# Skewness of 1024 rows: one reduce for two sums, two small ScalarE steps moved, and new transfer sizes

## Chip, cores, metric

One core of a Trainium2 chip. The metric is the device time of one execution in microseconds (us). All runs quoted here were fast (one core, granted TensorE clock 0.94 to 0.99).

Engines: PE is TensorE, PEld its weight loads, DVE is VectorE, ACT is ScalarE, POOL is GpSimd, SP is the queue that issues the transfers. In the profile lines, a bracket at the end names the idle time of the engine before the instruction and what ended it; `prof` prints it only where that idle time is above 0.15 us.

## The reference

```python
# x: 1024 x 8192 float32
mean = np.mean(x, axis=-1, keepdims=True)
std = np.std(x, axis=-1, keepdims=True)
z = (x - mean) / (std + 1e-8)
return np.mean(z ** 3, axis=-1)
```

The kernel gets it from three raw sums a row: of x, of x squared and of x cubed. 1024 rows are 8 blocks of 128 rows, numbered 0 to 7. A block is loaded in several transfers, called units here and counted from 0, as in the code (the prediction counts them from one: its "unit six" is unit 5).

## The kernel before

```python
UNITS = [                                    # columns of each transfer, by block
    [4096, 4096], [4096, 4096], [4096, 4096], [4096, 4096],
    [3072, 2944, 2176],
    [2944, 2688, 2560],
    [1664, 1536, 1664, 1792, 1536],
    [1024, 1152, 768, 1024, 1024, 1280, 1024, 896],
]
X_BUFS = 8                                   # so many transfers may be in flight or in use
...
s2u = small("s2u", NB * K); s3u = small("s3u", NB * K)     # partial sums, a column a slice
...
    def first_sums():                        # blocks 0 to 5, run in block 6
        for dst, src in ((m2a, s2u), (m3a, s3u)):
            v.tensor_reduce(out=dst, in_=src[:, 0 : F * K].rearrange("p (b c) -> p b c", c=K),
                            axis=X_AXIS, op=ALU.add)
        ...                                  # small ScalarE and GpSimd steps
    at(F - 2, 0, lambda: v.tensor_tensor(    # first means, in block 4
        out=m1a[:, 0:nw], in0=s1ps[:, 0:nw], in1=s1a, op=ALU.add))
    ...
    def mid_sums():                          # block 6, run in block 7: two reduces again
        ...
    def third_1(o):                          # "v"
        act(out=o["v3"], in_=o["m1sq"], func=AF.Identity, scale=-2.0 / 3.0, bias=o["m2"])
    def third_2(o):                          # "t"
        act(out=o["t"], in_=o["v3"], func=AF.Identity, scale=o["nm1"], bias=o["m3"])
    at(L, 4, lambda: third_1(mid))           # after unit 4 of the last block
    at(L, 5, lambda: third_2(mid))           # after unit 5
    at(L, 5, lambda: g.tensor_tensor(out=skew[:, F : F + 1], ...))

    for b, widths in enumerate(UNITS):
        for k, w in enumerate(widths):
            ...
            loads.append(nc.sync.dma_start(out=xt, in_=xv[b, :, c0 : c0 + w]))
            for s, e in _slices(b, w):
                ...
                act(out=sq, in_=xt[:, s:e], func=AF.Square, scale=s_scale,
                    accum_out=s2u[:, j : j + 1])                       # squares: ScalarE
                v.scalar_tensor_tensor(out=cube, in0=sq, scalar=1.0, in1=xt[:, s:e],
                    op0=ALU.mult, op1=ALU.mult, accum_out=s3u[:, j : j + 1])   # cubes: VectorE
            ...
            for c in range(n):                                         # sum of x: TensorE
                nc.tensor.matmul(out=tp, lhsT=xt[:, c * P : (c + 1) * P], rhs=ident,
                                 ..., is_transpose=True)
            for fn in todo.pop((b, k), ()):
                fn()                                                   # the small steps above
    copy_sums(L)                             # last block: ScalarE copy, then closing formulas
    ...
    third_2(o)
    v.tensor_scalar(out=skew[:, L:NB], in0=s3u[:, j - 1 : j], scalar1=o["t"], scalar2=o["rr"],
                    op0=ALU.add, op1=ALU.mult)                         # the last instruction
```

Of the kernel before, what the change touches and what calls it, by code (L numbers as in the profile page):

```python
# [10 lines left out]
ALU = mybir.AluOpType  # L11
# [3 lines left out]
X_AXIS = mybir.AxisListType.X  # L15
# [2 lines left out]
UNITS = [  # L18
    [4096, 4096],
    [4096, 4096],  # L20
    [4096, 4096],
    [4096, 4096],
    [3072, 2944, 2176],
    [2944, 2688, 2560],
    [1664, 1536, 1664, 1792, 1536],
    [1024, 1152, 768, 1024, 1024, 1280, 1024, 896],
]
S1_ACT = {(0, 0): 1024, (1, 0): 1024, (2, 0): 1024}
SUB_MAX = 2304
# [7 lines left out]
def _slices(b, w):  # L37
    n = -(-w // (SUB_WIDE if b >= 2 and w >= WIDE else SUB_MAX))
    step = -(-w // n // 128) * 128
    return [(s, min(s + step, w)) for s in range(0, w, step)]  # L40
# [3 lines left out]
def kernel(  # L44
# [5 lines left out]
    nc = tc.nc  # L50
# [5 lines left out]
    NB = R // P  # L56
    L = NB - 1
    F = EARLY
# [4 lines left out]
    nw = len(S1_ACT)  # L63
# [7 lines left out]
    n_sl = [sum(len(_slices(b, w)) for w in u) for b, u in enumerate(UNITS)]  # L71
    K = max(n_sl)
# [7 lines left out]
    def small(name, n):  # L80
        return onep.tile([P, n], FP, tag=name, name=name)
# [4 lines left out]
    nc.scalar.activation(out=tiny, in_=onesn, func=AF.Square)  # L86
    ident = small("ident", P)
    make_identity(nc, ident)
    s2u = small("s2u", NB * K)
    s3u = small("s3u", NB * K)  # L90
    nc.vector.memset(s2u, 0.0)
    nc.vector.memset(s3u, 0.0)
    s1a = small("s1a", nw)
    same = small("same", max(S1_ACT.values()))
    junk = small("junk", K)
# [7 lines left out]
    act, g, v = nc.scalar.activation, nc.gpsimd, nc.vector  # L103
# [4 lines left out]
    def at(b, k, fn):  # L108
        todo.setdefault((b, k), []).append(fn)
# [9 lines left out]
    for b in range(L):  # L119
# [1 line left out]
        at(b + 1, 0, lambda b=b: mean(b))  # L121


    m2a, m3a, m1sqa, m1sq3a, nm1a, vara, rra = (
        small(f"{t}a", F) for t in ("m2", "m3", "m1sq", "m1sq3", "nm1", "var", "rr")
    )

    def first_sums():
        for dst, src in ((m2a, s2u), (m3a, s3u)):
            v.tensor_reduce(  # L130
                out=dst, in_=src[:, 0 : F * K].rearrange("p (b c) -> p b c", c=K),
                axis=X_AXIS, op=ALU.add,
            )
        nc.scalar.copy(out=m1a[:, nw:F], in_=s1ps[:, nw:F])
        act(out=m1sqa, in_=m1a, func=AF.Square)
        g.tensor_tensor(out=vara, in0=m2a, in1=m1sqa, op=ALU.subtract)  # L136
        g.tensor_tensor(out=rra, in0=vara, in1=expo, op=ALU.pow)  # L137

    def first_rest():
# [4 lines left out]
        g.tensor_tensor(out=m3a, in0=m3a, in1=m1sq3a, op=ALU.add)  # L144
        g.tensor_tensor(out=skew[:, 0:F], in0=m3a, in1=rra, op=ALU.mult)  # L145

    at(F - 2, 0, lambda: v.tensor_tensor(
        out=m1a[:, 0:nw], in0=s1ps[:, 0:nw], in1=s1a, op=ALU.add))
    at(F, 1, first_sums)
    at(F, 2, first_rest)  # L150


    names = ("m2", "m3", "m1sq", "nm1", "var", "v3", "rr", "t")
    mid, end = ({t: small(f"{t}_{b}", 1) for t in names} for b in (F, L))

    def mid_sums():
        for t, src in (("m2", s2u), ("m3", s3u)):
            v.tensor_reduce(
                out=mid[t], in_=src[:, F * K : F * K + n_sl[F]], axis=X_AXIS, op=ALU.add
            )  # L160

    def mid_power():
        act(out=mid["m1sq"], in_=s1ps[:, F : F + 1], func=AF.Square)
# [4 lines left out]
    def third_1(o):  # L168
        act(out=o["v3"], in_=o["m1sq"], func=AF.Identity, scale=-2.0 / 3.0, bias=o["m2"])  # L169

    def third_2(o):
        act(out=o["t"], in_=o["v3"], func=AF.Identity, scale=o["nm1"], bias=o["m3"])  # L172

    at(L, 0, mid_sums)
    at(L, 1, mid_power)
    at(L, 4, lambda: third_1(mid))
    at(L, 5, lambda: third_2(mid))
    at(L, 5, lambda: g.tensor_tensor(  # L178
        out=skew[:, F : F + 1], in0=mid["t"], in1=mid["rr"], op=ALU.mult))

    for b, widths in enumerate(UNITS):
# [3 lines left out]
        for k, w in enumerate(widths):  # L185
# [4 lines left out]
            for s, e in _slices(b, w):  # L190
                if last_unit:
                    sq = psum1.tile([P, e - s], FP, tag="sqps", name="sqps")
                else:
                    sq = sqpool.tile([P, e - s], FP, tag="sq", name=f"sq_{b}_{k}_{s}")
                act(  # L195
                    out=sq, in_=xt[:, s:e], func=AF.Square, scale=s_scale,
# [4 lines left out]
                    out=cube, in0=sq, scalar=1.0, in1=xt[:, s:e],  # L201
# [4 lines left out]
            if w_act:  # L206
                act(  # L207
                    out=same[:, 0:w_act], in_=xt[:, w - w_act : w], func=AF.Copy,
# [3 lines left out]
            for c in range(n):  # L212
                nc.tensor.matmul(  # L213
                    out=tp, lhsT=xt[:, c * P : (c + 1) * P], rhs=ident,
# [10 lines left out]
    def row_sum(out, src, n):  # L225
# [13 lines left out]
        out=skew[:, L:NB], in0=s3u[:, j - 1 : j], scalar1=o["t"], scalar2=o["rr"],  # L239
# [37 lines left out]
```

## Time and profile before

| | before |
|---|---|
| median of the runs | 91.14 us (91.05 to 91.33, 6 runs) |
| span of the profiled run | 89.4 us |
| DVE, ACT busy | 73.5, 72.6 us |
| last transfer's landing | 83.66 us |
| ScalarE copy of the last block starts | 84.93 us |
| last cube ends | 86.53 us |
| last instruction starts | 86.85 us |

The landings in this document are read from the semaphore records of the trace; no view prints them, but a ScalarE start that waited for a transfer follows its landing by 0.08 us (unit 5: landing 81.33, start 81.41). Since the end hangs on the last landing and that moves by some tenths between executions, most comparisons below count from it: copy at +1.27, end of the last cube at +2.87, last instruction at +3.19 us. Times are taken to 0.01 us, so a difference of two can be off by 0.01.

The two pairs of reduces, which the change touches, in the VectorE timeline of before (start, length, instruction):

```profile
71.37 0.20 DVE L130 TENSOR_REDUCE m2a<-s2u 128x6 f32<-128x48 f32 x1
71.48 0.19 DVE L130 TENSOR_REDUCE m3a<-s3u 128x6 f32<-128x48 f32 x1
71.59 1.88 DVE L200 SCALAR_TENSOR_TENSOR sq<-sq,x 128x1664 f32<-128x1664 f32 x1
73.40 0.08 DVE L200 DVE_READ_ACCUMULATOR sq<-sq,x 128x1 f32 x1
73.53 2.03 DVE L200 SCALAR_TENSOR_TENSOR sq<-sq,x 128x1792 f32<-128x1792 f32 x1
...
78.31 0.15 DVE L158 TENSOR_REDUCE m<-s2u 128x1 f32<-128x5 f32 x1
78.38 0.15 DVE L158 TENSOR_REDUCE m<-s3u 128x1 f32<-128x5 f32 x1
78.44 1.35 DVE L200 SCALAR_TENSOR_TENSOR sq<-sq,x 128x1152 f32<-128x1152 f32 x1
```

A pair costs from its first start to the start of what follows: 0.22 and 0.13 us. A cube that waits for nothing starts together with the accumulator read of the cube ahead (as at 77.16, 79.71 and 80.59 in this trace). So the cube at 73.53 could have started at 73.40; it waited for its square.

### The profile page before, as it was taken

To read this page: it belongs to the slowest core of one execution; us is meant where nothing else is said; L and a number is where in the kernel's file an instruction comes from. 1 tells how busy PE (TensorE), PEld (TensorE's weight loads), DVE (VectorE), ACT (ScalarE), POOL (GpSimd) and SP (SyncE) were. 2 spreads that over 40 slices of the span, in tenths; PEclk is the share of its full clock that TensorE was granted. 3 is DMA by queue.
4 is the path that set the end of the run, shared out by engine and by line. 5 is a ranking of instruction groups with operands and counts; after the bars stand their busy time and mean duration, and the time that the engine had idled before them with its cause. 6 is when DMAs were issued, how large, how long until landed. Compare 5 with 4: busy or idle time off the path is not lost.

```text
span 89.4 us, 1405 instructions
## 1 busy us (share of the span) xinstructions
PE 62.8 (70%) x504; PEld 58.0 (65%) x504; DVE 73.5 (82%) x97; ACT 72.6 (81%) x120; POOL 13.7 (15%) x18
## 2 busy tenths in 40 slices
PE   0003989492790925999999699489897889897810
PEld 0003969391790915999999598479796778865710
DVE  1000498989989497999989999999999999999980
ACT  6003999599990999989799899499899989998960
POOL 3000000000000000000000000000000089999730
PEclk9999999999999998589999999999999999999999
DMA  4899999999999999999999999999999999996000
GB/s 117 330 403 462 425 425 440 425 425 440 425 433 418 425 433 432 425 433 411 425 424 410 428 435 412 408 429 411 417 416 417 413 406 411 413 403 236 8 0 2
DMA packets 4038, 33.64 MB, mean 376 GB/s; under 512 B 576, under 2 KB 576, under 8 KB 2240
## 3 DMA queue, kind: packets, MB, share of 16 engines
q1 hardware_dynamic: 4032, 33.56, 90.2%
q8 instruction: 4, 0.07, 0.3%
q14 instruction: 2, 0.02, 0.0%
HBM read 33.55 MB, written 0.00 MB: 375 GB/s over the span
## 4 chain that ended last, share of the span: by engine, by line
DMA 58%; DVE 19%; ACT 14%; issue 5%; SPq 1%; PE 0%; ACTq 0%; DVEq 0%
DMA x<-in_x_dram 58%; DVE sq L200 18%; ACT sq L195 9%; ACT same L207 1%; ACT sqps L195 1%; SPq L188 1%; ACT t L172 1%; ACT tsb L112 0%; PE s1ps L115 0%; DVE skew L238 0%; ACT v L169 0%; ACT junk L226 0%; ACT m1sq L231 0%; DVE m2a L130 0%; DVE m3a L130 0%
## 5 line engine op out<-in xcount | busy, mean ns | idle before, releaser
L200 DVE SCALAR_TENSOR_TENSOR sq<-sq,x 128x1408 f32<-128x1408 f32 (+9 forms) x43 | 71.7, 1721 | 12.6 <-ACT sq L195 12.4
L195 ACT ACTIVATE sq<-x 128x1408 f32<-128x1408 f32 (+9 forms) x43 | 62.3, 1451 | 13.1 <-DMA x<-in_x_dram 12.4
L213 PE MATMUL tp<-ident,x 128*128 128x128 f32 x488 | 60.9, 284 | 15.2 <-DMA x<-in_x_dram 15.0
L213 PEld LDWEIGHTS tp<-ident,x 128*128 128x128 f32 x488 | 56.6, 148 | 18.2 <-DMA x<-in_x_dram 10.0
L136 POOL TENSOR_TENSOR vara<-m2a,m1sqa 128x6 f32<-128x6 f32 x1 | 1.8, 1812 | 70.4 <-DVE m3a L130 70.4
L115 PEld LDWEIGHTS s1ps<-onesn,tsb 128*128 128x128 f32 x16 | 2.4, 188 | 9.3 <-ACT tsb L112 9.3
L115 PE MATMUL s1ps<-onesn,tsb 128*128 128x1 f32 x16 | 3.0, 255 | 7.6 <-ACT tsb L112 7.6
L195 ACT ACTIVATION_READ_ACCUMULATOR sq<-x 128x1 f32 x43 | 8.0, 187 | 0.0
L200 DVE DVE_READ_ACCUMULATOR sq<-sq,x 128x1 f32 x43 | 3.6, 83 | 0.0
L137 POOL TENSOR_TENSOR rra<-vara,expo 128x6 f32<-128x6 f32 x1 | 3.1, 3145 | 0.1
L207 ACT ACTIVATE same<-x 128x1024 f32<-128x1024 f32 x3 | 3.1, 1041 | 0.0
L112 ACT COPY tsb<-tp 128x128 f32<-128x128 f32 x8 | 1.9, 242 | 0.0
L86 ACT ACT_TABLE_LOAD x1 | 1.3, 1283 | 0.7 <-PEq L261 0.7
L166 POOL TENSOR_TENSOR rr<-var,expo 128x1 f32<-128x1 f32 x1 | 1.4, 1426 | 0.1
L144 POOL TENSOR_TENSOR m3a<-m3a,m1sq3a 128x6 f32<-128x6 f32 x1 | 1.3, 1330 | 0.1
L165 POOL TENSOR_TENSOR var<-m,m1sq 128x1 f32<-128x1 f32 x1 | 1.2, 1174 | 0.0
L200 DVE SCALAR_TENSOR_TENSOR cube<-sqps,x 128x896 f32<-128x896 f32 x1 | 1.1, 1089 | 0.0
L143 POOL TENSOR_TENSOR m1sq3a<-m1sq3a,nm1a 128x6 f32<-128x6 f32 x1 | 1.1, 1067 | 0.1
L178 POOL TENSOR_TENSOR skew<-t,rr 128x1 f32<-128x1 f32 x1 | 1.0, 976 | 0.1
L195 ACT ACTIVATE sqps<-x 128x896 f32<-128x896 f32 x1 | 0.9, 897 | 0.0
L145 POOL TENSOR_TENSOR skew<-m3a,rra 128x6 f32<-128x6 f32 x1 | 0.8, 799 | 0.1
L172 ACT ACTIVATE t<-v,m,nm 128x1 f32<-128x1 f32 x2 | 0.8, 379 | 0.0
(36 smaller groups left out, 7.5 us busy)
## 6 DMA issues: line engine op xcount, KB each, us to landing
x<-in_x_dram SPq DMA_DIRECT2D x8, 2048.0 KB, 23.4
x<-in_x_dram SPq DMA_DIRECT2D x2, 1472.0 KB, 29.6
x<-in_x_dram SPq DMA_DIRECT2D x4, 512.0 KB, 8.4
x<-in_x_dram SPq DMA_DIRECT2D x2, 832.0 KB, 18.4
x<-in_x_dram SPq DMA_DIRECT2D x1, 1536.0 KB, 32.5
x<-in_x_dram SPq DMA_DIRECT2D x2, 768.0 KB, 16.1
x<-in_x_dram SPq DMA_DIRECT2D x1, 1344.0 KB, 25.0
x<-in_x_dram SPq DMA_DIRECT2D x1, 1280.0 KB, 23.0
```

The source lines that it names most:

```text
L86: nc.scalar.activation(out=tiny, in_=onesn, func=AF.Square)
L112: nc.scalar.copy(out=Tsb[b % 2], in_=tps[b])
L115: nc.tensor.matmul(out=s1ps[:, b : b + 1], lhsT=Tsb[b % 2], rhs=onesn, start=True, stop=True)
L136: g.tensor_tensor(out=vara, in0=m2a, in1=m1sqa, op=ALU.subtract)
L137: g.tensor_tensor(out=rra, in0=vara, in1=expo, op=ALU.pow)
L144: g.tensor_tensor(out=m3a, in0=m3a, in1=m1sq3a, op=ALU.add)
L166: g.tensor_tensor(out=mid["rr"], in0=mid["var"], in1=expo[:, 0:1], op=ALU.pow)
L172: act(out=o["t"], in_=o["v3"], func=AF.Identity, scale=o["nm1"], bias=o["m3"])
L195: act(out=sq, in_=xt[:, s:e], func=AF.Square, scale=s_scale, accum_out=s2u[:, j : j + 1],)
L200: v.scalar_tensor_tensor(out=cube, in0=sq, scalar=1.0, in1=xt[:, s:e], op0=ALU.mult, op1=ALU.mult, accum_out=s3u[:, j : j + 1],)
L207: act(out=same[:, 0:w_act], in_=xt[:, w - w_act : w], func=AF.Copy, scale=inv_n, accum_out=s1a[:, b : b + 1],)
L213: nc.tensor.matmul(out=tp, lhsT=xt[:, c * P : (c + 1) * P], rhs=ident, start=(k == 0 and c == 0), stop=(c0 == C and c == n - 1), is_transp ...
```

## The change

Its intent: fewer VectorE instructions, small steps where their engine has time, and transfer sizes that let both engines follow the loads more closely at the end.

```diff
-    [4096, 4096],                       # block 2
+    [3456, 3712, 1024],
     [4096, 4096],
-    [3072, 2944, 2176],
-    [2944, 2688, 2560],
-    [1664, 1536, 1664, 1792, 1536],
-    [1024, 1152, 768, 1024, 1024, 1280, 1024, 896],
+    [3200, 2816, 2176],
+    [2944, 2816, 2432],
+    [1792, 1792, 1664, 1664, 1280],
+    [896, 1024, 1280, 1024, 1024, 1152, 1024, 768],
...
-    s2u = small("s2u", NB * K)
-    s3u = small("s3u", NB * K)
-    nc.vector.memset(s2u, 0.0)
-    nc.vector.memset(s3u, 0.0)
+    sums = small("sums", 2 * NB * K)
+    nc.vector.memset(sums, 0.0)
+    s2u, s3u = sums[:, 0 : NB * K], sums[:, NB * K :]
...                                      # first_sums; mid_sums likewise
-        for dst, src in ((m2a, s2u), (m3a, s3u)):
-            v.tensor_reduce(out=dst, in_=src[:, 0 : F * K]..., axis=X_AXIS, op=ALU.add)
+        v.tensor_reduce(out=m23a.rearrange("p (m b) -> p m b", m=2),
+                        in_=by_block[:, :, 0:F, :], axis=X_AXIS, op=ALU.add)
...
-    at(F - 2, 0, lambda: v.tensor_tensor(
+    at(nw, 0, lambda: v.tensor_tensor(  # first means, in block 3
...
-    at(L, 4, lambda: third_1(mid))
-    at(L, 5, lambda: third_2(mid))
-    at(L, 5, lambda: g.tensor_tensor(
+    at(L, 3, lambda: third_1(mid))
+    at(L, 4, lambda: third_2(mid))
+    at(L, 4, lambda: g.tensor_tensor(
```

More of the change, by code (lines that the diff above doesn't have):

```diff
@@ L121 @@
         at(b + 1, 0, lambda b=b: mean(b))
-    m2a, m3a, m1sqa, m1sq3a, nm1a, vara, rra = (
-        small(f"{t}a", F) for t in ("m2", "m3", "m1sq", "m1sq3", "nm1", "var", "rr")
-    )
+    m1sqa, m1sq3a, nm1a, vara, rra = (
+        small(f"{t}a", F) for t in ("m1sq", "m1sq3", "nm1", "var", "rr")
+    )
+    m23a = small("m23a", 2 * F)
+    m2a, m3a = m23a[:, 0:F], m23a[:, F:]
+    by_block = sums.rearrange("p (m b c) -> p m b c", m=2, c=K)
     def first_sums():
-        for dst, src in ((m2a, s2u), (m3a, s3u)):
-            v.tensor_reduce(
-                out=dst, in_=src[:, 0 : F * K].rearrange("p (b c) -> p b c", c=K),
-                axis=X_AXIS, op=ALU.add,
-            )
+        v.tensor_reduce(
+            out=m23a.rearrange("p (m b) -> p m b", m=2), in_=by_block[:, :, 0:F, :],
+            axis=X_AXIS, op=ALU.add,
+        )
         nc.scalar.copy(out=m1a[:, nw:F], in_=s1ps[:, nw:F])
@@ L154 @@
     mid, end = ({t: small(f"{t}_{b}", 1) for t in names} for b in (F, L))
+    m23m = small("m23m", 2)
+    mid["m2"], mid["m3"] = m23m[:, 0:1], m23m[:, 1:2]
     def mid_sums():
-        for t, src in (("m2", s2u), ("m3", s3u)):
-            v.tensor_reduce(
-                out=mid[t], in_=src[:, F * K : F * K + n_sl[F]], axis=X_AXIS, op=ALU.add
-            )
+        v.tensor_reduce(
+            out=m23m, in_=by_block[:, :, F, 0 : n_sl[F]], axis=X_AXIS, op=ALU.add
+        )
     def mid_power():
```

## The prediction

> **What bounds the kernel now.** I read the page first (busy shares, the 40 slices), then the chain that ended last, then the timelines of VectorE (DVE) and ScalarE (ACT), then the landing of each transfer from the semaphore records behind the sync queue.
>
> Busy shares and the slices of the page:
>
> ```profile
> PE 62.8 (70%) x504; PEld 58.0 (65%) x504; DVE 73.5 (82%) x97; ACT 72.6 (81%) x120; POOL 13.7 (15%) x18
> DVE  1000498989989497999989999999999999999980
> DMA  4899999999999999999999999999999999996000
> GB/s 117 330 403 462 425 425 440 425 425 440 425 433 418 425 433 432 425 433 411 425 424 410 428 435 412 408 429 411 417 416 417 413 406 411 413 403 236 8 0 2
> ```
>
> The load stream never pauses, from 2 us to about 82 us. The DVE is full from the middle to the end. So two things are close to their limits at once: the bytes (33.55 MB) and the cubes on the DVE. Neither is touched by the change: the bytes stay, and the cubes stay 44 instructions over 65,536 columns.
>
> The chain that ended last, its last pieces (start, length, what):
>
> ```profile
> 73.55 7.78 DMA x<-in_x_dram
> ...
> 81.41 1.25 ACT sq L195
> ...
> 82.68 0.37 ACT t L172
> 83.05 1.04 ACT sq L195 x2
> 84.09 0.93 ACT sqps L195 x2
> 85.02 0.16 ACT tsb L112
> ...
> 86.37 0.40 ACT t L172
> ...
> 86.85 0.27 DVE skew L238
> ```
>
> The end is set by the landing of the sixth unit of the last block (81.33 us), then by ScalarE back to back: three squares, block 6's last step "t" between them, and the closing formulas.
>
> The same stretch in the timeline, ACT and DVE (start, length, engine, line, operation, idle before):
>
> ```profile
> 80.88 0.28 ACT L169 ACTIVATE v<-m1sq,m 128x1 f32<-128x1 f32 x1
> 81.41 1.27 ACT L195 ACTIVATE sq<-x 128x1280 f32<-128x1280 f32 x1 [0.26 <-DMA x<-in_x_dram]
> 82.68 0.37 ACT L172 ACTIVATE t<-v,m,nm 128x1 f32<-128x1 f32 x1
> 84.93 0.24 ACT L112 COPY tsb<-tp 128x128 f32<-128x128 f32 x1
> 85.44 1.09 DVE L200 SCALAR_TENSOR_TENSOR cube<-sqps,x 128x896 f32<-128x896 f32 x1
> 86.45 0.09 DVE L200 DVE_READ_ACCUMULATOR cube<-sqps,x 128x1 f32 x1
> 86.85 0.27 DVE L238 TENSOR_SCALAR skew<-s3u,t,rr 128x1 f32<-128x1 f32 x1 [0.31 <-ACT t L172]
> ```
>
> The reader is to see that two chains reach the last instruction within 0.3 us: ScalarE's "t" ends at 86.76, the DVE's last cube at 86.54. A gain on one alone is worth at most that 0.3 us. After 86.85 come 0.27 us of work and some 2.3 us of storing and closing that stay.
>
> **What the Trainium skill says.** (1) "VectorE: DVE Perf Modes", section "The TRN2 errata": an SBUF operation pays a fixed cost per instruction, and a fp32 two-input operation of 2048 columns takes 2291 ns; here a cube of 2048 columns takes 2.29 us, so it agrees. Start to start the cubes stand closer, 2.22 us for 2048 columns and 1.15 for 1024, that is 1.04 ns a column and about 0.08 us an instruction. (2) Same page, "The perf-mode tier table": tensor_reduce has one element a cycle and nothing faster. The trace agrees: 48 elements take 0.20 us, 5 take 0.15, about 1.1 ns each. So one reduce over both halves saves a fixed part only, not elements. (3) "Perfetto Trace Analysis", section "Roofline": a single core is bounded by its 16 DMA engines at about 435 GB/s; the stretch from 10 to 45 us moved 427, that from 45 to 75 us 418. No change of issue order can do much against that. (4) "DMA: Bandwidth & Descriptors", section "Why a DMA increments its semaphore by 16 and not by 1": up to 16 engines finish independently and all are counted. Here the rate falls to 236 GB/s in the slice that ends at 82.7 us while the last unit lands only at 83.66: the slowest engine decides.
>
> **The change part by part.**
>
> *Reduces.* In the first sums the two reduces start at 71.37 and 71.48 and the next cube at 71.59: 0.22 us for the pair. One of 96 elements is 0.11 plus 48 x 1.04 ns, 0.16: saves 0.06. For block 6 the pair runs from 78.31 to 78.44, 0.13 us; one of 10 elements is 0.08: saves 0.05. The memset at the start (0.11 us) ends 9 us before the DVE's first cube: saves nothing. In the order of instructions no new wait between engines appears from the two halves now lying in one tile.
>
> *First means in block 3.* The add (0.08 us start to start, at 53.03) moves to about 45 us. The DVE idles there 0.25 us until the second unit of block 3 is squared, so it is free at its new place. But at its old place it was hidden too: the DVE waits again at 58.75 to 58.87 for block 5's first unit. Worth nothing.
>
> *Transfers.* From ScalarE starts that a landing released: 38.77 and 43.67, 4096 columns in 4.90 us; 78.54 and 79.82, 1024 columns in 1.28. So a transfer costs about 0.07 us plus 1.18 ns a column. The 28th adds 0.07 us: the last landing goes from 83.66 to 83.73. Instruction counts of squares and cubes stay (block 2 three and three, block 3 to 7 the same), and eight buffers still keep more than 6 us of loads in flight (a late load lands 6.4 us or more after its issue).
>
> *DVE chain.* Block 5's first unit lands at the same column, 0.07 us later: the DVE starts it at 58.94 instead of 58.87. Blocks 5, 6 and 7 are the same 24,576 columns in the same 19 cubes. Before, one wait of 0.12 us (start of the fourth unit of block 6, 73.53 instead of 73.41) lay among them. With 1792, 1792, 1664, 1664, 1280 the DVE reaches that unit at about 73.85 and its square is ready at about the same time (landing 72.05, plus 0.08, 1.58 and 0.12). So this wait mostly goes. Sum for the end of the last cube: +0.07 - 0.06 - 0.05 - 0.10 = -0.14, that is 86.40 instead of 86.54.
>
> *ScalarE chain.* Last landings: 83.73; less 0.98 for 768 columns, 82.75; less 1.28, 81.47. Unit six starts at 81.55, and 1152 columns take 1.17 (76.29 to 77.46): 82.72. Block 6's "t", 0.28 us start to start at 82.68 before, now sits one unit earlier, where ScalarE waits for a landing anyway (0.26 us idle before 81.41), so it leaves the path. Its "v" moves likewise into the wait ahead of unit five. Unit seven starts at its landing, 82.83, ends at 83.87; the last of 768 takes 0.93 - 0.11 = 0.82: 84.69 against 84.93, that is -0.24. But the copy also needs TensorE: 25 transposes took 3.32 us from 81.37, 0.133 each. The last 6 now start at 83.85, behind unit seven's, and end with the last one's latency at about 84.8. So the copy comes 0.13 to 0.24 earlier, taken as 0.17. The 1.92 us from copy to last instruction stay.
>
> *Sum.* The last instruction starts at the later of ScalarE's 86.85 - 0.17 = 86.68 and the DVE's 86.40 plus its release: 86.68. So **91.15 - 0.17 = 90.98 us**, 0.2% less.
>
> **The rivals.** (a) *The DVE takes over as the last.* The reduce over both halves is a strided access and follows a wait on the DVE's own count; if that costs 0.1 us each, and if the fourth unit of block 6 still waits, the cubes end at 86.6 to 86.7 and nothing or 0.1 us is gained: 91.05 to 91.15. For: the DVE has no idle time from 59 us on. Against: the second reduce of the old pair has the same kind of wait and starts 0.07 to 0.11 us after the first. (b) *The landings shift.* Block 2's first unit landed 1.5 us later than its size explains (26.66 to 29.14: ScalarE idle 2.38 us), and all later landings keep that delay. Instruction fetches share the DMA engines. If other sizes move such a delay, everything after moves by some tenths, either way: 90.6 to 91.5. Nothing in the diff aims at it. (c) *A deeper gain:* with several waits gone, 0.3 to 0.4 us. Against: both chains stand on the landings near the end, which are fixed by bytes. (d) *Block 6's steps end later on GpSimd*, since the first sums come about 0.5 us later with 1792 columns as second unit; GpSimd then ends block 6 at about 84.9 and is needed again at about 85.7: hidden.
>
> **Range and chances.** The three times of before span 0.18 us. The gain is between 0 and 0.4 from (a) and (c), with (b) on either side: range 90.72 to 91.28. A change of 2% is 1.8 us, ten times what is on any path here; only a new stall of the loads could do that. Faster 0.01, same 0.98, slower 0.01.
>
> **What would show it right or wrong.** Right: "t" of block 6 stands in the idle time before unit six; ScalarE's copy starts 0.13 to 0.24 us earlier and the last DVE instruction about as much; one reduce takes about 0.06 us less than its pair; the last landing is within 0.1 us of 83.66; no ScalarE idle time names the DVE. Wrong: the last instruction waits for the cube instead of "t"; the wait in block 6 stays or grows; or the landing of block 5's first unit (57.2) has moved by more than 0.2 us, in which case the transfers decide and not the small operations.

## The result and the profile after

90.90 us median (90.81 to 91.09, 6 runs) against 91.14 of before; ratio 0.9971, 95% interval 0.9957 to 0.9985. A ratio is the mean time of one kernel's fast runs over that of the other's of the same rounds, so not quite the ratio of the medians. The change is below 2%, so it counts as "same", but it is clear of the noise. 90.98 was predicted, with 90.72 to 91.28 as range.

The last pieces of the chain after (start, length, what):

```profile
79.95 0.18 ACT v L171
80.14 1.04 ACT sq L197 x2
81.18 0.28 ACT t L174
...
81.51 1.19 ACT sq L197 x2
...
82.75 1.15 ACT sq L197 x2
83.90 0.83 ACT sqps L197 x2
84.72 0.16 ACT tsb L111
...
86.07 0.40 ACT t L174
...
86.56 0.27 DVE skew L240
```

"t" now stands at 81.18, ahead of unit 5's square, and nothing stands between the last three squares. The chain goes through "t" here and not through a landing, because "t" just fills the wait: it ends at 81.46, unit 5 landed at 81.43, and its square starts 0.08 us after the landing, as it does in the kernel before. In the kernel before, "v" stood in a wait already (80.88, with unit 5's square at 81.41); it moves up because "t" needs its result.

The timeline of the same stretch and of the reduces (ACT and DVE):

```profile
81.09 0.37 ACT L174 ACTIVATE t<-v,m23m,nm 128x1 f32<-128x1 f32 x1
81.51 1.17 ACT L197 ACTIVATE sq<-x 128x1152 f32<-128x1152 f32 x1
82.75 1.06 ACT L197 ACTIVATE sq<-x 128x1024 f32<-128x1024 f32 x1
84.63 0.24 ACT L111 COPY tsb<-tp 128x128 f32<-128x128 f32 x1
...
71.77 0.25 DVE L131 TENSOR_REDUCE m23a<-sums 128x12 f32<-128x96 f32 x1
71.94 1.88 DVE L202 SCALAR_TENSOR_TENSOR sq<-sq,x 128x1664 f32<-128x1664 f32 x1
73.74 0.08 DVE L202 DVE_READ_ACCUMULATOR sq<-sq,x 128x1 f32 x1
73.74 1.88 DVE L202 SCALAR_TENSOR_TENSOR sq<-sq,x 128x1664 f32<-128x1664 f32 x1
...
77.98 0.16 DVE L160 TENSOR_REDUCE m23m<-sums 128x2 f32<-128x10 f32 x1
78.05 1.21 DVE L202 SCALAR_TENSOR_TENSOR sq<-sq,x 128x1024 f32<-128x1024 f32 x1
...
85.32 0.95 DVE L202 SCALAR_TENSOR_TENSOR cube<-sqps,x 128x768 f32<-128x768 f32 x1
86.56 0.27 DVE L240 TENSOR_SCALAR skew<-sums,t,rr 128x1 f32<-128x1 f32 x1 [0.27 <-ACT t L174]
```

The one reduce costs 0.17 us start to start instead of 0.22, that of block 6 0.07 instead of 0.13, and the cube at 73.74 follows the one before without a wait. The copy comes 0.30 us earlier (84.63), the last cube ends at 86.28 (before 86.53), and the last instruction, which still waits for ScalarE's "t", starts at 86.56, 0.29 us earlier. The last landing in this run is 83.61. From the landing: copy +1.02 (was +1.27), last cube +2.67 (was +2.87), last instruction +2.95 (was +3.19).

### The profile page after: what moved, and what is told of

It is laid out like the page before. It is cut to its first block, busy times and chain, and to the rows that moved or that the text cites. A ratio compares the mean times of both kernels' runs of the same rounds, so it can differ in the third digit from the quotient of the medians.

```text
span 89.1 us, 1404 instructions
## 1 busy us (share of the span) xinstructions
PE 64.2 (72%) x504; PEld 58.5 (66%) x504; DVE 73.3 (82%) x94; ACT 72.8 (82%) x120; POOL 13.1 (15%) x18
## 4 chain that ended last, share of the span: by engine, by line
DMA 70%; ACT 12%; DVE 5%; PE 3%; issue 3%; SPq 3%; ACTq 0%; DVEq 0%
DMA x<-in_x_dram 70%; ACT sq L197 9%; DVE sq L202 5%; PE tp L215 3%; SPq L190 3%; ACT sqps L197 1%; ACT t L174 1%; PE s1ps L114 1%; ACT v L171 1%; ACT tsb L111 0%; DVE skew L240 0%; ACT junk L228 0%; ACT m1sq L233 0%; ACT nm L236 0%; ACTq L197 0%
## 5 line engine op out<-in xcount | busy, mean ns | idle before, releaser
L215 PE MATMUL tp<-ident,x 128*128 128x128 f32 x488 | 61.8, 286 | 13.3 <-DMA x<-in_x_dram 13.0
L137 POOL TENSOR_TENSOR vara<-m23a,m1sqa 128x6 f32<-128x6 f32 x1 | 1.7, 1700 | 70.8 <-DVE m23a L131 70.8
L146 POOL TENSOR_TENSOR skew<-m23a,rra 128x6 f32<-128x6 f32 x1 | 1.3, 1334 | 0.1
L167 POOL TENSOR_TENSOR var<-m23m,m1sq 128x1 f32<-128x1 f32 x1 | 1.2, 1177 | 0.0
L145 POOL TENSOR_TENSOR m23a<-m23a,m1sq3a 128x6 f32<-128x6 f32 x1 | 1.1, 1134 | 0.1
L202 DVE SCALAR_TENSOR_TENSOR cube<-sqps,x 128x768 f32<-128x768 f32 x1 | 1.0, 951 | 0.0
L197 ACT ACTIVATE sqps<-x 128x768 f32<-128x768 f32 x1 | 0.8, 797 | 0.0
```

What stands on the lines that cost most here:

```text
L137: g.tensor_tensor(out=vara, in0=m2a, in1=m1sqa, op=ALU.subtract)
L146: g.tensor_tensor(out=skew[:, 0:F], in0=m3a, in1=rra, op=ALU.mult)
L197: act(out=sq, in_=xt[:, s:e], func=AF.Square, scale=s_scale, accum_out=s2u[:, j : j + 1],)
```

## The experiments

Three theories. **A**: the end hangs on ScalarE's stretch after the last landings, with VectorE close behind; the gain is "t" leaving that stretch, and the smaller last unit. **B**: the gain is the shorter VectorE work (reduces). **C**: the gain comes from where the transfers land.

All runs gave correct results. Each was compared with runs of the kernel before on the same chip. The table has the profiled run of each (us; the last three columns count from its last landing):

```
run                    median  ratio to before, 95%        landing  copy  cube end  last instr.
before                 91.14   -                           83.66   +1.27  +2.87     +3.19
changed                90.90   0.9971 (0.9957 to 0.9985)   83.61   +1.02  +2.67     +2.95
k1_steps_only          90.98   0.9986 (0.9972 to 1.0001)   83.70   +1.07  +2.86     +3.02
k2_units_only          91.15   1.0002 (0.9990 to 1.0014)   83.71   +1.20  +2.79     +3.12
k3_reduce_only         91.10   1.0003 (0.9988 to 1.0018)   83.69   +1.32  +2.84     +3.24
k4_means_only          91.28   1.0014 (0.9999 to 1.0030)   83.89   +1.28  +2.85     +3.19
k5_after_old_steps     91.23   0.9990 (0.9971 to 1.0008)   83.78   +1.19  +2.67     +3.11
k6_after_old_reduce    91.03   0.9969 (0.9952 to 0.9987)   83.69   +1.02  +2.77     +2.94
k7_dve_plus            91.16   0.9984 (0.9965 to 1.0002)   83.85   +1.03  +2.87     +3.02
k8_dve_plus_more       91.53   1.0039 (1.0025 to 1.0054)   84.02   +1.01  +3.29     +3.44
k9_act_plus            91.31   1.0006 (0.9986 to 1.0026)   83.70   +1.35  +2.71     +3.27
k10_tail_nine          90.94   0.9978 (0.9965 to 0.9991)   83.64   +0.85  +2.68     +2.82
k11_tail_eight         91.19   1.0005 (0.9989 to 1.0022)   83.73   +1.13  +2.69     +3.06
k12_steps_last_block   91.01   0.9984 (0.9970 to 0.9999)   83.81   +1.05  +2.85     +3.00
```

The intervals are about 0.15% wide to each side and the effects are of that size, so single ratios between 0.998 and 1.000 settle little; the positions in the traces carry the argument. They are one execution a kernel. How well they repeat shows in ScalarE's copy, where kernels with the same ScalarE work and sizes in the last block serve as repeats: old steps and old sizes +1.27, +1.28, +1.32 (before, k4, k3); old steps and new sizes +1.20, +1.19 (k2, k5); new steps and new sizes +1.02, +1.02, +1.03, +1.01 (changed, k6, k7, k8), with k12 at +1.05. The kernels ran on two chips (k5, k6, k7 and k9 on one where the kernel before had a median of 91.29 us), so compare their ratios, not their medians.

### One part alone, on the kernel before

**k1_steps_only**

```diff
-    at(L, 4, lambda: third_1(mid))      # and third_2 and the GpSimd step at (L, 5)
+    at(L, 3, lambda: third_1(mid))      # and those at (L, 4)
```

> The kernel before with one change: block 6's two late ScalarE steps one unit earlier. Theory A (the end hangs on ScalarE's last stretch, and the gain is the step 't' leaving it): the ScalarE copy starts 0.15 to 0.25 us earlier than 84.93, the last instruction then waits for 't' or the last cube, which still ends at about 86.54, so it starts at 86.60 to 86.70 instead of 86.85; time -0.15 to -0.25 us, ratio about 0.998. Theory B (the gain is the shorter VectorE work): nothing, ratio 1.000. Theory C (the gain comes from where the transfers land): nothing, ratio 1.000.

From the landing, copy and last instruction came 0.20 and 0.17 us earlier (+1.07 and +3.02); the ratio, 0.9986, agrees in size but its interval just reaches 1. The timeline of this run, ScalarE and VectorE:

```profile
80.88 0.37 ACT L172 ACTIVATE t<-v,m,nm 128x1 f32<-128x1 f32 x1
...
85.48 1.08 DVE L200 SCALAR_TENSOR_TENSOR cube<-sqps,x 128x896 f32<-128x896 f32 x1
86.72 0.27 DVE L238 TENSOR_SCALAR skew<-s3u,t,rr 128x1 f32<-128x1 f32 x1
```

"t" has left the last stretch. At the end the two chains now tie. The last instruction (86.72) starts 0.10 us after the closing "t" ends (86.61), which is what it takes in before and changed, where it waits for "t"; and it starts 0.15 us after the last cube's end (86.56), which is what it takes in k7 and k8 below, where VectorE is clearly the last (0.14 to 0.15; no run goes below). So the rest of what ScalarE gained can't show.

**k2_units_only**: the diff's `UNITS` alone.

> The kernel before with the new 28 transfers alone, block 6's steps after units 4 and 5 as before. Theory A: 't' again stands behind the sixth unit's square, so only the smaller last unit helps: copy about 0.10 us earlier, time -0.1 us, ratio 0.999. The last cube ends about 0.15 us earlier than 86.54 (no wait in block 6), which does not show. Theory B: nothing or -0.05 us. Theory C: all of the gain, -0.24 us, ratio 0.997, with the last landing as in the changed kernel (83.6).

Copy and last instruction 0.07 us earlier from the landing (+1.20, +3.12), and VectorE's last cube 0.08. The landing itself, 83.71, is not earlier. The time shows nothing (1.0002). That is theory A's small share, slightly less than it expected, and not theory C's 0.24 us. It is seen in the traces alone, hardly above their scatter of 0.05 us, but twice (k2, k5).

**k3_reduce_only**: the diff's `sums`, `m23a` and `m23m` with one reduce each.

> The kernel before with one tile for both sums and one reduce for both, nothing else. Theory A: the last cube ends about 0.1 us earlier and the last instruction still waits for ScalarE: no change, ratio 1.000. Theory B: -0.1 to -0.2 us, ratio 0.998 to 0.999. Theory C: nothing.

Nothing (1.0003; last instruction at +3.24). The cubes end only 0.03 us earlier: in this kernel the wait in block 6 remains (the cube starts at 73.56 instead of 73.41), and it eats what the first reduce saves. Theory B falls.

**k4_means_only**

```diff
-    at(F - 2, 0, lambda: v.tensor_tensor(
+    at(nw, 0, lambda: v.tensor_tensor(
```

> The kernel before with only the add of the first means moved from block 4 to block 3. All theories: nothing, ratio 1.000 within 0.1 per cent; the add falls into a VectorE wait of 0.25 us at about 45 us, and the 0.08 us it frees at 53 us lengthens the VectorE wait before 58.87 from 0.11 to about 0.2 us.

Nothing: 1.0014 with 1 inside the interval by a hair, and the last instruction at +3.19 as before. What makes this profiled run longer is the last landing, 83.89.

### One part undone, on the changed kernel

**k5_after_old_steps**: the diff of k1 reversed.

> The changed kernel with block 6's two steps back after units 4 and 5. Theory A: 't' stands on ScalarE's path again, behind the sixth unit: copy 0.15 to 0.25 us later than the changed kernel's 84.63, time +0.15 to +0.2 us on it, ratio to the kernel before about 0.999. Theories B and C: as fast as the changed kernel, ratio 0.997.

```profile
82.83 0.37 ACT L174 ACTIVATE t<-v,m23m,nm 128x1 f32<-128x1 f32 x1
...
86.89 0.27 DVE L240 TENSOR_SCALAR skew<-sums,t,rr 128x1 f32<-128x1 f32 x1 [0.43 <-ACT t L174]
```

"t" is back behind unit 5, copy and last instruction are 0.17 and 0.16 us later than in the changed kernel (+1.19, +3.11), the cubes are not (+2.67). VectorE now waits 0.43 us for ScalarE. Theory A.

**k6_after_old_reduce**: the two tiles and the two reduces each back, the rest of the change kept.

> The changed kernel with the two separate reduces and tiles back. Theory A: the last cube ends about 0.1 us later (86.4 instead of 86.28), still before ScalarE's 't' at 86.46: no change against the changed kernel, ratio to the kernel before 0.997. Theory B: most of the gain is lost, ratio 0.999 to 1.000. Theory C: 0.997.

The cubes end 0.10 us later (+2.77), the last instruction does not (+2.94), and the time keeps the whole gain: 0.9969. The merged reduces do what they should on VectorE and are worth nothing here. Theory B falls a second time. (With +2.77 the cube is nearly the last: the room that the next runs measure is used up but for some hundredths.)

### How much room each chain has

**k7_dve_plus** and **k8_dve_plus_more**: a useless VectorE add of 128, or of 512, columns ahead of the last cube.

```diff
+    padi, pado = small("padi", 512), small("pado", 512)
+    nc.gpsimd.memset(padi, 1.0)
+    at(L, 6, lambda: v.tensor_tensor(
+        out=pado[:, 0:128], in0=padi[:, 0:128], in1=padi[:, 0:128], op=ALU.add))   # k8: 512
```

> The changed kernel with a useless VectorE add of 128 columns (about 0.2 us) ahead of the last cube. Theory A: VectorE has 0.2 us or slightly more to spare: last cube ends at 86.48, the last instruction starts 0 to 0.05 us later, ratio to the kernel before 0.997 to 0.9975. Theory B: +0.2 us, ratio 0.9993.

> The changed kernel with a useless VectorE add of 512 columns (about 0.6 us) ahead of the last cube. Theory A: the last cube ends at 86.9 and becomes the last to be waited for: the last instruction starts at about 86.95 instead of 86.56, time +0.35 to +0.4 us, not +0.6. Theory B: +0.6 us.

```profile
85.57 0.28 DVE L185 TENSOR_TENSOR pado<-padi 128x128 f32<-128x128 f32 x1
85.78 0.95 DVE L206 SCALAR_TENSOR_TENSOR cube<-sqps,x 128x768 f32<-128x768 f32 x1
...
86.87 0.27 DVE L244 TENSOR_SCALAR skew<-sums,t,rr 128x1 f32<-128x1 f32 x1
```

In k7 the add takes 0.21 us (85.57 to 85.78) and the last instruction comes 0.07 us later from the landing (+3.02 against +2.95). In k8 the last cube ends 0.62 us later and the last instruction 0.49. Both give the same room: 0.14 and 0.13 us. I had expected about 0.2 to 0.27. The reason is the 0.14 to 0.15 us between the end of the last cube and the last instruction that depends on it, which is there in every run where VectorE decides (k7, k8, k10, k12) and in the tie of k1: 86.56 - 86.28 leaves 0.28, less 0.14 is 0.14. The timed cost of k8, 1.0039 over the changed kernel's 0.9971, is 0.6 us, more than the 0.49 of the trace; its landing was late as well (84.02). That delay came up at block 4's second unit, which landed at 51.36 us (50.96 in the changed kernel, though block 3's last unit had landed at 43.61 against 43.72), 34 us before the added instruction runs. The same unit is late in kernels without the added instruction too: by the rate that fits the other landings (0.07 us and 1.18 ns a column) by 0.18 us in the kernel before and 0.28 in k1, against 0.52 in k8, 0.27 in k7 and 0.01 in the changed kernel. And the other three runs of k8 were 0.27 to 0.42 us faster than the profiled one (91.44 to 91.59 against 91.86). Why the unit is late is open.

**k9_act_plus**: a useless ScalarE square of 256 columns ahead of the last unit's square.

```diff
+    at(L, 6, lambda: act(out=pado[:, 0:256], in_=padi[:, 0:256], func=AF.Square))
```

> The changed kernel with a useless ScalarE square of 256 columns (about 0.3 us start to start) ahead of the last unit's square. Theory A: all of it shows: copy, 't' and last instruction about 0.3 us later, time +0.3 us, ratio to the kernel before 1.000 to 1.001. Theory B: less than 0.1 us shows. Theory C: nothing shows.

```profile
83.92 0.40 ACT L185 ACTIVATE pado<-padi 128x256 f32<-128x256 f32 x1
84.22 0.80 ACT L200 ACTIVATE sqps<-x 128x768 f32<-128x768 f32 x1
```

It takes 0.30 us start to start, and copy and last instruction come 0.33 and 0.32 us later from the landing. The ratio went from 0.9971 to 1.0006. ScalarE has no room at all in this stretch.

### Other sizes in the last block

**k10_tail_nine** and **k11_tail_eight**, on the changed kernel:

```diff
-    [896, 1024, 1280, 1024, 1024, 1152, 1024, 768],
+    [1024, 1024, 1024, 896, 896, 1024, 896, 768, 640],     # k10
+    [1152, 1280, 1280, 1152, 896, 1024, 768, 640],         # k11
```

> The changed kernel with nine units in the last block, the last 1024, 896, 768, 640. Theory A: ScalarE's square of a unit then takes no longer than the next unit's landing, and the last square is 128 columns shorter: copy about 0.17 us earlier than 84.63; VectorE pays one more instruction (0.08 us), last cube at about 86.36, just in time: time -0.1 to -0.17 us on the changed kernel, ratio to the kernel before 0.9955. Theory B: +0.08 us, ratio 0.998. Theory C: the 29th transfer costs up to 0.07 us, ratio 0.998.

> The changed kernel with eight units in the last block, the last 896, 1024, 768, 640. Theory A: copy about 0.10 us earlier, VectorE unchanged: time -0.1 us on the changed kernel, ratio to the kernel before 0.996. Theories B and C: no change, 0.997.

k10: the copy came 0.17 us earlier from the landing (+0.85), as expected, and the last instruction 0.13 (+2.82), because the cubes now decide (the last instruction starts 0.14 us after the last cube, 0.13 after "t"). By the clock the expectation missed: 0.9955 was expected, outside the interval of 0.9965 to 0.9991, and no gain can be told: 90.94 us and 0.9978 against 90.90 and 0.9971, measured in different sets of runs. So it is not shown to beat the changed kernel.

k11 missed: the copy is later, not earlier (+1.13). By the clock nothing is left of the gain (1.0005, 0.9989 to 1.0022); in the trace 0.11 of the 0.24 us is lost (+3.06). Its ScalarE timeline suggests why (read from one trace, not tested by a further run):

```profile
80.88 0.28 ACT L171 ACTIVATE v<-m1sq,m23m 128x1 f32<-128x1 f32 x1
81.06 0.94 ACT L197 ACTIVATE sq<-x 128x896 f32<-128x896 f32 x1
82.00 0.37 ACT L174 ACTIVATE t<-v,m23m,nm 128x1 f32<-128x1 f32 x1
```

Unit 4 landed at 80.75, but the square of unit 3 (1152 columns) and "v" held ScalarE until 81.06, so it entered unit 4 0.31 us after the landing instead of 0.08; "t" then held back unit 5, which had landed at 82.03 and started at 82.27. The expectation mentions neither step. The same two steps, in the same places in the program, are free or cost time depending on whether a wait for a landing follows them. That fits theory A.

**k12_steps_last_block**: the kernel before with the steps moved (k1) and only the last row of `UNITS` new.

> The kernel before with block 6's steps one unit earlier and the new sizes in the last block alone; blocks 2 to 6 and the reduces as before. Measured from the last landing, since that moves by some tenths between executions. ScalarE: as in the changed kernel, copy 1.02 us after the last landing (before: 1.27). VectorE: if the new sizes of block 6 matter (they took away a wait of 0.05 to 0.12 us), the last cube ends about 0.1 us later than in the run with old reduces, 2.85 to 2.90 us after the last landing, and decides: last instruction 3.0 to 3.05 us after the last landing, time -0.15 us on the kernel before, ratio 0.998. If they don't, 2.94 us and ratio 0.997.

ScalarE's copy is nearly that of the changed kernel (+1.05), but the last cube ends at +2.85 and the last instruction follows 0.15 us behind it (+3.00; 0.13 behind "t"), as expected if the sizes of block 6 matter. The run with old reduces (k6) has +2.77 and +2.94. So the new sizes in the blocks before, which took away the wait in block 6, seem to matter by about 0.06 us (one trace each): without them VectorE is the last. (k6 also has the moved first means, which k4 shows to be worth nothing.)

## Why the prediction was right

The time was 0.08 us below the predicted one, within the range, and the class was as forecast. Point by point:

- **"t" and "v" move into waits.** Right, and it is the main part. Moving them alone gives -0.17 us from the landing (k1), moving them back costs +0.16 (k5). "t" stands in the idle time before unit 5 as foretold, with nothing to spare.
- **Sizes.** The rest, -0.07 us, is what the new units give alone (k2), also foretold (a last square shorter by 0.11). Together -0.24, and the trace of the changed kernel shows -0.24. (On the copy it is 0.20 and 0.07 against 0.25. The clock can't confirm the split: k2 alone is 1.0002, 0.9990 to 1.0014.)
- **Copy.** Predicted at about 84.76 with the landing at 83.73, that is +1.03; measured +1.02. That the two agree so well is partly luck, because the reasoning was half wrong. ScalarE alone was to be ready at 84.69 (+0.96), and the rest was laid to TensorE. But TensorE's last transpose ended at 84.53, 0.10 us before the copy, and the copy starts 0.09 us after ScalarE's accumulator read ahead of it, as in the kernel before: ScalarE alone set it, 0.06 us later than its sum said. Only in k1, with 7 transposes in the last unit, does TensorE seem to hold the copy, by 0.03 us (last transpose to 84.73, copy at 84.77; ends on TensorE are modelled).
- **The 28th transfer.** It was to cost 0.07 us at the last landing. It can't be seen: the nine kernels with the new or further units landed between 83.61 and 84.02, the five with the old sizes in blocks 0 to 6 between 83.66 and 83.89. Both groups have the mean 83.75. So in this pair the sum missed here: without the term the predicted -0.17 becomes -0.24 us. It does not show that a transfer costs nothing: by the fit of 0.07 us a transfer and 1.18 ns a column, the last landing came 1.32 us later than its columns and transfers explain in the kernel before and 1.16 in the changed one (estimates from the landings of the traces). Delays of that kind, which nothing in the change aims at, are larger than the term and can hide it.
- **Reduces.** 0.05 and 0.06 us less a pair, as predicted (0.06 and 0.05); off the path, as predicted. In k6 the pairs cost VectorE 0.10 us and the time nothing.
- **First means.** Worth nothing, as predicted (k4).
- **VectorE's end.** Predicted 86.40, measured 86.28. All of the difference is the landing of block 5's first unit, 57.12 instead of the predicted 57.24 (57.17 and 0.07): from it to the end of the last cube 29.16 us were predicted, and 29.16 measured (before: 29.36).
- **The rivals.** (a) VectorE as the last: not in the changed kernel, but only 0.14 us away (k7, k8); it is the last in k10 and k12 and level with ScalarE in k1. (b) Landings that shift: they do, by up to 0.4 us from one kernel's execution to another's, but not with the change. (c) The deeper gain: no. (d) GpSimd: it ended block 6 at 84.29 and was needed at 85.59, hidden.

## What to carry to other kernels

When an engine follows a stream of loads, it is the order of its small steps against the landings that counts: a step of 0.2 to 0.3 us is free where a long enough wait for a load follows it, and costs most or all of its length just behind the last ones (here 0.16 to 0.20 us for the 0.28 of "t" in k1 and k5, and all 0.30 of k9's square). Ask of every small step which wait follows it, and how much room that leaves when the sizes are changed. When two chains end within 0.3 us of each other, find the room of each by adding a known useless instruction. An engine that has room left gains nothing from savings on it (here VectorE, with 0.14 us of room, from the merged reduces). And compare from the last landing, since that moves by more than the effect.

## What the Trainium skill lacked or had wrong

- No page has a number for what a dependent VectorE instruction waits after its producer. "VectorE: DVE Perf Modes", section "The DRAIN you can't avoid", says for a chain of copies that the semaphore costs nothing extra. Here an independent cube starts 0.07 to 0.08 us before the record of the cube ahead ends (before: a cube from 84.30 to 85.52, the next at 85.44), while the last instruction, which needs the last cube, starts 0.14 to 0.15 us after its end in the four runs where "t" had ended early enough (k7, k8, k10, k12). That is some 0.2 us between the two.
- "Runtime: NRT & Kernel Launch", section "Instruction fetch mechanics", calls the fetch of 16 KiB blocks mostly hidden. The trace agrees on the size (four packets of 16,384 bytes) and shows each holding a DMA engine for 0.9 to 1.1 us. In all 14 traces the first, starting between 26.6 and 27.3 us, falls into the delivery of the unit that lands latest for its size, by 1.0 to 1.7 us (block 2: landing 29.06 in the kernel before, 32.70 in the changed one), and the later landings keep that delay. That the fetch is the cause was not tested.
